# Three expert layers: token rows by indirect DMA throughout, TensorE's products of a pair in a written order, and the overflow branch moved ahead of the pairs

## The chip, the cores and the metric

The kernel runs on one core of a Trainium2 chip (trn2). The metric is the device time of one execution in microseconds (us), taken as the median of several runs; lower is better. All inputs and the output are 32-bit floats.

## What is computed

Two transformer blocks and a third one on a batch of 256 latent and 256 context tokens, 1024 wide. Each block is a mixer (attention or convolution) followed by a layer of 32 experts. The three expert layers are what the change touches:

```python
def hier_moe(h, w_group, b_group, w_expert, b_expert, w1, w3, w2):
    ...
    e_prob, e_idx = lax.top_k(jax.nn.softmax(le, axis=-1), TOP_K)
    weights = g_prob * e_prob / jnp.sum(e_prob, axis=-1, keepdims=True)
    expert_id = g_idx * EXPERTS_PER_GROUP + e_idx
    ...
    def expert_block(args):
        xb, e = args
        return (jax.nn.silu(xb @ w1[e]) * (xb @ w3[e])) @ w2[e]
    ...
    return jnp.zeros_like(h).at[stok].add(y)
```

A token goes to two experts of one group. Each expert multiplies its tokens' rows by W1 and W3 (1024 x F), takes silu(first) times second, multiplies by W2 (F x 1024), and its result, weighted, is added to the token; a gate vector scales the sum before the residual add. The first layer (moe0) has 512 tokens and F = 512, the second (moe1) 256 tokens and F = 512, the third (moe2) 256 tokens and F = 256.

## The kernel before, in words

The program runs mixer_ab, moe0, mixer_c, moe1, a third mixer and moe2 one after the other. `moe` (from L583) does one expert layer, with T = 4 or 2 tiles of 128 tokens. `make_hT` makes the normed, transposed tokens; `route` (L695) makes the router's choice, a rank of each token within its expert (TensorE products at L727, L728 and L734 into bank O), and from it the table `slot`: for each of 16 pairs of experts 128 slots (64 for each expert, `CAP`), each with a token's number and its weight. `warm` (L254) issues products whose result nobody reads.

Then come 16 turns of `pair` (L834), one for each pair of experts. Expert 0 of the pair sits in columns 0 to 63 of TensorE, expert 1 in columns 64 to 127, so that W1, W3 and W2 products run in a tile mode 64 columns wide (`128*64` in the rows below). All others (transposes, one-hot products) use the full `128*128` mode. One pair is: W1 and W3 products (`up`, L845, into the two `pj` banks), silu on ScalarE (L853), the elementwise product on VectorE (L855), its transposes (L861, bank O) and their copy (L218 on VectorE or L220 on ScalarE in turn), W2 products (L875, banks PT), a split of the weighted result into a high and a low part (L880 on ScalarE, L881 on VectorE), and `combine`: one-hot products that take the 128 slots back to the tokens (L888, 2 for each tile of tokens and half of the row, into the two banks S), the gate on VectorE (L890) and the add to the residual `xs` (L891, GpSimd for one half of the row and VectorE for the other).

How a pair gets its rows depends on the layer. In moe0 an indirect DMA on GpSimd's queue (`gather_rows`, L642) fetches the 128 slots' rows from a copy `hd` in DRAM into one half of tile `xg`, two pairs ahead, and `turn` (L650) transposes them on TensorE in 8 pieces through bank acc. In moe1 and moe2 `gather` (L808) makes one-hot matrices on VectorE (L816, L817) and multiplies them with the tokens in a high and a low part on TensorE (L824, for two pairs at a time), and scales while copying out (L225, L227).

The order on an engine is that of a list scheduler that simulates the program. `combine` of a pair is a generator; the next pair calls it through `fill` between its own products (after every 8 of W1 and W3, 2 times ahead of the transposes, 8 times ahead of W2), and the scheduler then moves the single products further, so L888 and L845 stand mixed on TensorE.

The weights come as loads of 1 MB on SyncE's queue (L200), 12 for a pair in moe0 and moe1, 6 in moe2, in the order of their use, into a cycle of buffers (7 of tag w, 7 of tag x in moe0 and 6 in the others, 1 of tag r). A load waits until the products that read its buffer are done; 11 loads (moe0) or 13 are issued ahead of the pairs.

Behind the 16 pairs stands `rest` (L896): a value is loaded into the registers of all engines (`over`, L899), and a branch (L900) enters a loop for experts that have more than 64 tokens. On these inputs it is not entered.

## Time and profile before

| what | value |
|---|---|
| median of 3 runs | 2130.99 us (2127.89 to 2133.66) |
| the profiled execution's own time | 2128.83 us |
| its span in the trace | 2126.8 us |
| mean granted TensorE clock | 0.969 |
| TensorE products busy | 1944.7 us, 91% of the span |
| TensorE weight loads busy | 998.4 us, 47% |
| VectorE, ScalarE, GpSimd busy | 1025.1, 472.5, 475.1 us |
| DMA | 635.23 MB, mean 299 GB/s |
| loops over pairs: moe0, moe1, moe2 | about 375 to 888, 1198 to 1687, 1841 to 2114 us |

Busy is the time in which an engine had an instruction of its kind running. The granted clock is a share of full speed: 1.00 is 2.4 GHz, 0.50 is 1.2 GHz. The DMA share is how much of the time the core's 16 DMA engines had packets under way; it can come out slightly above 1. The share of a whole span is an average over stages with different limits, so the rows below are cut to the three loops and to what lies between them.

### The profile page before, as it was taken

How to read it: one execution, taken by the hardware profiler on the slowest of the kernel's cores; microseconds unless marked ns; L12 is line 12 of the kernel's file. 1: busy time of each engine (PE TensorE's matmuls, PEld its weight loads, DVE VectorE, ACT ScalarE, POOL GpSimd, SP SyncE). 2: the span in 40 equal slices, each digit the busy share in tenths (PEclk: the TensorE clock that was granted, in tenths of full speed). 3: DMA queues.
4: the chain of work that ended last, by engine and by line, in shares of the span. 5: the costliest groups of instructions: out<-in, count | busy, mean ns of one | idle time of the engine just before them, and what ended most of it. 6: DMA issues, size and time to landing. Idle time of an engine off the chain costs nothing. (4 is left out here: it accounts for less than half of the span.)

```text
span 2126.8 us, 25665 instructions
## 1 busy us (share of the span) xinstructions
PE 1944.7 (91%) x9834; PEld 998.4 (47%) x9834; DVE 1025.1 (48%) x2174; ACT 472.5 (22%) x978; POOL 475.1 (22%) x387
## 2 busy tenths in 40 slices
PE   5999997999999999889988999999999797999997
PEld 2865455333333333378855533333333274555553
DVE  4567655244443434566577333322323376454544
ACT  3346522110000000133342211101111136211111
POOL 3421331121212211354244100001000125111111
PEclk7999998999999999899999999999999999999999
DMA  8645566899999999334366699999999722698882
GB/s 335 248 170 190 179 237 246 337 419 417 393 394 383 386 386 399 130 104 164 134 251 227 276 420 422 421 420 383 406 405 388 282 77 111 241 396 353 362 365 92
DMA packets 111650, 635.23 MB, mean 299 GB/s; under 512 B 12328, under 2 KB 32024, under 8 KB 40848
## 3 DMA queue, kind: packets, MB, share of 16 engines
q1 hardware_dynamic: 104608, 618.57, 73.2%
q0 software_dynamic: 4640, 8.70, 1.2%
q10 hardware_dynamic: 2256, 6.09, 0.8%
q8 instruction: 83, 1.36, 0.3%
q14 instruction: 63, 0.52, 0.1%
HBM read 634.23 MB, written 3.27 MB: 300 GB/s over the span
## 5 line engine op out<-in xcount | busy, mean ns | idle before, releaser
L891 POOL TENSOR_TENSOR xs<-xs,m 128x512 f32<-128x512 f32 x128 | 170.9, 1335 | 1031.6 <-DVE m L890 1023.2
L845 PE MATMUL pj<-w,a 128*64 128x512 f32 (+1 forms) x1592 | 381.2, 529 | 3.5 <-DVE a L225 2.8
L845 PE MATMUL pj<-x,a 128*64 128x512 f32 (+1 forms) x1296 | 331.8, 526 | 2.1 <-DVE a L225 2.1
L247 PE MATMUL pj<-w,x 128*128 128x256 f32 (+1 forms) x1728 | 285.3, 309 | 7.2 <-DVE x L234 3.0
L890 DVE TENSOR_TENSOR m<-S,bc 128x512 f32<-128x512 f32 x256 | 169.4, 684 | 179.3 <-PE S L888 176.6
L247 PEld LDWEIGHTS pj<-w,x 128*128 128x128 f32 x1728 | 230.0, 192 | 50.6 <-issue 30.1
L845 PEld LDWEIGHTS pj<-w,a 128*64 128x64 f32 x1592 | 132.5, 137 | 179.8 <-issue 154.3
L881 DVE SCALAR_TENSOR_TENSOR j<-PT,slot,j 128x512 fp32r<-128x512 f32 x96 | 71.7, 749 | 264.5 <-ACT j L880 260.4
L875 PE MATMUL PT<-x,a 128*64 128x512 f32 x608 | 185.5, 614 | 7.3 <-DVE a L218 4.3
L888 PE MATMUL S<-j,a 128*128 128x512 f32 x512 | 176.5, 443 | 16.8 <-DVE m L890 12.8
L845 PEld LDWEIGHTS pj<-x,a 128*64 128x64 f32 x1296 | 114.6, 136 | 143.8 <-issue 124.6
L875 PE MATMUL PT<-w,a 128*64 128x512 f32 x576 | 162.4, 608 | 7.9 <-DVE a L218 4.4
L855 DVE TENSOR_TENSOR a<-a,pj 128x512 f32<-128x512 f32 (+1 forms) x48 | 42.9, 894 | 232.6 <-PE pj L845 232.6
L888 PEld LDWEIGHTS S<-j,a 128*128 128x128 f32 x512 | 83.1, 190 | 147.0 <-issue 58.2
L880 ACT ACTIVATE j<-PT,slot 128x512 fp32r<-128x512 f32 x96 | 66.0, 687 | 386.4 <-PE PT L875 383.7
L891 DVE TENSOR_TENSOR xs<-xs,m 128x512 f32<-128x512 f32 x128 | 120.9, 945 | 2.5
L853 ACT ACTIVATE a<-pj 128x512 f32<-128x512 f32 (+1 forms) x48 | 25.3, 526 | 379.6 <-PE pj L845 379.6
L875 PEld LDWEIGHTS PT<-x,a 128*64 128x64 f32 x608 | 58.1, 139 | 91.4 <-issue 78.6
L875 PEld LDWEIGHTS PT<-w,a 128*64 128x64 f32 x576 | 51.2, 138 | 85.1 <-issue 70.5
L824 PEld LDWEIGHTS S<-a,x 128*128 128x128 f32 x512 | 64.4, 189 | 34.6 <-issue 11.6
L824 PE MATMUL S<-a,x 128*128 128x256 f32 x512 | 76.3, 293 | 3.0 <-DVE a L817 1.2
L263 POOL TENSOR_TENSOR sj<-sj,neghalf 128x8 f32<-128x8 f32 (+3 forms) x30 | 46.2, 1543 | 133.8 <-DVE sj L262 124.4
(363 smaller groups left out, 2430.8 us busy)
## 6 DMA issues: line engine op xcount, KB each, us to landing
w<-in_w_dram SPq DMA_DIRECT2D x189, 1024.0 KB, 9.1
x<-in_w_dram SPq DMA_DIRECT2D x170, 1024.0 KB, 10.0
x<-in_w_mod_dram SPq DMA_DIRECT2D x28, 1024.0 KB, 8.1
r<-in_w_dram SPq DMA_DIRECT2D x25, 1024.0 KB, 9.5
r<-in_w_mod_dram SPq DMA_DIRECT2D x20, 1024.0 KB, 4.9
w<-in_w_gate_e_dram SPq DMA_DIRECT2D x17, 1024.0 KB, 10.7
w<-in_w_up_e_dram SPq DMA_DIRECT2D x16, 1024.0 KB, 7.7
w<-in_w_down_e_dram SPq DMA_DIRECT2D x16, 1024.0 KB, 10.6
```

The lines of the kernel that those rows point to most:

```text
L247: self.nc.tensor.matmul(out, a[x], b[y], start=first and i == 0, stop=last and i == len(terms) - 1)
L263: self.nc.gpsimd.tensor_tensor(out, ms, self.neghalf[:, :cols], op=OP.pow)
L824: nc.tensor.matmul(px[:, k, :], h(t)[i][:, (k0 + k) * 128:(k0 + k + 1) * 128], oh[:, t], start=t == i == 0, stop=t == T - 1 and i == 1)
L845: nc.tensor.matmul(ph[64 * e:64 * e + 64, :], xT(k, e), W(e, k), start=(k == 0), stop=(k == 7), tile_position=(0, 64 * e))
L853: nc.scalar.activation(s, p1, AF.Silu)
L855: nc.vector.tensor_tensor(a.rearrange("p (k q) -> p q k", k=nk), s.rearrange("p (q k) -> p q k", k=nk), p3.rearrange("p (q k) -> p q k", k ...
L875: nc.tensor.matmul(py[n][64 * e:64 * e + 64, :], aT[:, k, 64 * e:64 * e + 64], W2(e, k)[:, n * 512:(n + 1) * 512], start=(k == 0), stop=(k ...
L880: nc.scalar.activation(hi, py[n], AF.Copy, scale=slot[:, 1:2])
L881: nc.vector.scalar_tensor_tensor(lo, py[n], slot[:, 1:2], hi, op0=OP.mult, op1=OP.subtract)
L888: nc.tensor.matmul(po, back[:, t * 128:(t + 1) * 128], parts[n][i], start=(i == 0), stop=(i == 1))
L890: nc.vector.tensor_tensor(tmp, po, gate[:, n * 512:(n + 1) * 512], op=OP.mult)
L891: (nc.vector if n and (DVA or last) else nc.gpsimd).tensor_tensor(xn, xn, tmp, op=OP.add)
```

## The change

Rows: moe1 and moe2 fetch their rows by indirect DMA as well; the one-hot `gather` and all that fed it (`kp`, the high and low parts in `make_hT`) go. `route` hands back its work in pieces: the count `over` at once, then `ids` (the token numbers of all slots, tile `at`), then `weigh`; the table with the weights is built by `table`.

Branch: `rest` stands between the first two gathers and the 16 pairs. The branch is an edge that no instruction of an engine is moved across by the scheduler, and it put all gathers behind the branch.

Order: with `tc.keep_in_program_order` the products of a pair stand as written. With T = 2: W1, W3, the previous pair's combine (8 products, banks S, S, acc, O), the transposes, the turn of the next pair's rows, W2. With T = 4 the combine is cut in two, 8 products behind W1 and 8 behind W3. A change of mode is a step from `128*64` to `128*128` products or back.

Smaller parts: with T = 2 the gate is multiplied into the pair's result before the split, and VectorE adds the combine's bank straight to `xs`; the copy of the transposes is always ScalarE's; moe1 and moe2 issue 12 loads ahead in place of 13, and their cycle has 7 buffers of tag x.

```diff
-        self.cycle = ["w"] * TAGS["w"][1] + ["x"] * (TAGS["x"][1] - (T if T == 2 else 1)) + ["r"] * TAGS["r"][1]
+        self.cycle = ["w"] * TAGS["w"][1] + ["x"] * (TAGS["x"][1] - 1) + ["r"] * TAGS["r"][1]
...
+            ids()
+            xg = self.t("x").rearrange("p (b d) -> p b d", b=2)
+            nc.gpsimd.memset(xg, 0.0)
+        ahead(8 - T // 2 * (3 if T == 2 else 2))
...
+        for p in range(2):
+            gather_rows(self.at[:, p:p + 1], xg[:, p])
+        weigh()
         add = [(self.xs[:, t], gates[i // 2]) for i, t in enumerate(tiles)]
+        self.rest(m, T, inputs, over, experts, add)
+        xT = turn(xg[:, 0], "aa")
+        self.slot = self.cp.tile([128, 16, 2], F32, name=f"slot{m}", tag="slot")
+        self.table(T, 0, self.slot)
         done = iter(())
         for p in range(16):
-            if T == 2 and p and p % 2 == 0:
-                xT = pairs(p)
-            if T > 2:
-                if p + 2 < 16:
-                    gather_rows(self.slot[:, p + 2, 0:1], p % 2)
+            if p + 2 < 16:
+                gather_rows(self.at[:, p + 2:p + 3], xg[:, p % 2])
+            after = {}
+
+            def meanwhile():
                 if p + 1 < 16:
-                    xT[p + 1] = turn((p + 1) % 2)
...
+                    after["xT"] = turn(xg[:, (p + 1) % 2], pin=self.tc.keep_in_program_order)
...
         run(done)
-        self.rest(m, T, inputs, over, experts, add)
...
+        def ids():
             chosen(rank2, each(rank))
...
+            self.at = self.cp.tile([128, 16], I32, name=f"at{m}", tag="at")
+            nc.vector.tensor_scalar(self.at, self.tokens(T, R.rearrange("p w t e -> p (w t) e"), 0), -1.0, None, op0=OP.add)
...
+        pin = (lambda i: i) if lean else tc.keep_in_program_order
...
         p1 = up(W1)
         s, a = self.t("a2", FF), self.t("a2", FF)
         nc.scalar.activation(s, p1, AF.Silu)
+        if T > 2:
+            step()
         p3 = up(W3)
...
-        fill()
-        fill()
-        pa = self.p("O", FF).rearrange("p (k s) -> p k s", k=nk)
+        step()
+        pa = self.p("pj", FF).rearrange("p (k s) -> p k s", k=nk)
...
-        self.copy(aT, pa)
+        self.copy(aT, pa, "a")
+        meanwhile()
...
+        one = T == 2
         for n in range(2):
             hi, lo = parts[n]
-            nc.scalar.activation(hi, py[n], AF.Copy, scale=slot[:, 1:2])
-            nc.vector.scalar_tensor_tensor(lo, py[n], slot[:, 1:2], hi, op0=OP.mult, op1=OP.subtract)
+            if one:
+                y = self.t("m2")
+                nc.vector.scalar_tensor_tensor(y, py[n], slot[:, 1:2], add[0][1][:, n * 512:(n + 1) * 512], op0=OP.mult, op1=OP.mult)
+                nc.scalar.activation(hi, y, AF.Copy)
+                nc.vector.tensor_tensor(lo, y, hi, op=OP.subtract)
...
+            units = [(t, n) for t in range(T) for n in range(2)]
+            for u0 in range(0, 2 * T, 4):
+                run4 = list(zip(units[u0:u0 + 4], [self.p(b) for b in ("S", "S", "acc", "O")]))
+                for (t, n), o in run4:
                     for i in range(2):
...
+                        pin(nc.tensor.matmul(o, back[:, t * 128:(t + 1) * 128], parts[n][i], start=(i == 0), stop=(i == 1)))
```

On TensorE in moe1, inside W1 and W3 of one pair, the order before was as follows (pj_11007 is the bank of W1, pj_11039 that of W3, j the high and low parts, S the combine's bank; a `64x512` row is a product in the narrow mode):

```order
L845 MATMUL pj_11039<-w_10993,a_2599_10937 64x512
L845 MATMUL pj_11039<-w_10995,a_2600_10938 64x512
L845 MATMUL pj_11039<-w_10997,a_2600_10938 64x512
L845 MATMUL pj_11039<-w_10995,a_2600_10938 64x512
L888 MATMUL S_11016<-j_10903,a_2591_10899 128x512
L888 MATMUL S_11030<-j_10904,a_2591_10899 128x512
L888 MATMUL S_11030<-j_10905,a_2591_10899 128x512
L845 MATMUL pj_11039<-w_10997,a_2600_10938 64x512
L845 MATMUL pj_11039<-w_10995,a_2600_10938 64x512
L845 MATMUL pj_11039<-w_10997,a_2600_10938 64x512
L845 MATMUL pj_11039<-w_10995,a_2600_10938 64x512
L845 MATMUL pj_11007<-x_10985,a_2599_10937 64x512
```

The combine's rows L888 stand in the middle of a pair's products, in groups of 1 to 4. The same place of the changed kernel, behind 32 rows L812 of W1 and W3 (L862 is the combine, L827 the transposes, L635 the turn of the next pair's rows, L840 W2):

```order
L862 MATMUL S_12411<-j_12316,a_2920_12313 128x512
L862 MATMUL S_12411<-j_12317,a_2920_12313 128x512
L862 MATMUL S_12412<-j_12318,a_2920_12313 128x512
L862 MATMUL S_12412<-j_12319,a_2920_12313 128x512
L862 MATMUL acc_12413<-j_12316,a_2920_12313 128x512
L862 MATMUL acc_12413<-j_12317,a_2920_12313 128x512
L862 MATMUL O_12414<-j_12318,a_2920_12313 128x512
L862 MATMUL O_12414<-j_12319,a_2920_12313 128x512
L827 MATMUL pj_12427<-cst,a_2943_12391 128x128 x4
L635 MATMUL S_12435<-cst,x_10646 128x128 x4
L635 MATMUL S_12441<-cst,x_10646 128x128 x4
L840 MATMUL PT_12454<-r_12365,a_2950_12432 64x512
```

All products in the wide mode now stand in one piece between W3 and W2.

On TensorE at the start of moe1's pairs the order before was this (L824 is the one-hot gather of the first two pairs, L899 the load of `over`, L845 W1 of the first pair):

```order
L824 MATMUL S_10648<-a_2534_10626,x_10470 128x256
L824 MATMUL S_10648<-a_2534_10626,x_10471 128x256
L824 MATMUL S_10648<-a_2534_10626,x_10470 128x256
L824 MATMUL S_10648<-a_2534_10626,x_10471 128x256
L899 TENSOR_LOAD over_10689
L254 MATMUL acc_13763<-cst 128x512 x4
L845 MATMUL pj_10734<-w_10456,a_2535_10635 64x512
L845 MATMUL pj_10734<-w_10458,a_2535_10635 64x512
L824 MATMUL S_10659<-a_2534_10626,x_10470 128x256
```

The changed kernel has there, from the last row of the branch's body on (L885, L882 and L880 are the branch's own, L778 a part of the weight table, L635 the turn of the first rows, L812 W1 of the first pair):

```order
L862 MATMUL O_11264<-j_11226,a_2649_11220 128x512
L885 REGISTER_ALU
L885 COMPARE_AND_BRANCH
L885 UNCONDITIONAL_BRANCH
L882 UNCONDITIONAL_BRANCH
L880 UNCONDITIONAL_BRANCH
L778 MATMUL pj_11302<-j_11303,a_2670_11297 64x16 x8
L635 MATMUL S_11278<-cst,x_10646 128x128 x4
L635 MATMUL S_11284<-cst,x_10646 128x128 x4
L812 MATMUL pj_11317<-w_10451,a_2666_11277 64x512
```

The first pair's products now stand behind the branch and behind the turn, which reads what the first gather brings; on GpSimd's queue that gather (L627) also stands behind the branch (L880).

## Rows read from the trace of the kernel before

**Rows 1.** Windows: us, busy time of PE, PEld, DVE, ACT, POOL, granted clock, DMA share, GB/s
```profile
391.00:880.00 489.00, 466.32 (x1866) 171.38 (x1864) 200.63 (x321) 43.12 (x68) 95.68 (x73) 1.00 0.96 386
1215.00:1440.00 225.00, 211.50 (x916) 82.19 (x913) 73.86 (x132) 25.44 (x41) 17.91 (x14) 0.99 1.01 421
1440.00:1665.00 225.00, 209.16 (x882) 80.09 (x882) 71.73 (x125) 23.49 (x38) 20.44 (x16) 0.98 0.98 395
1850.00:2085.00 235.00, 226.03 (x1434) 125.77 (x1431) 118.99 (x238) 41.72 (x76) 33.32 (x26) 1.00 0.90 367
```

**Rows 2.** Timeline of PE in the first loop: start, us, then idle before and releaser
```profile
642.78 7.09 PE L845 MATMUL pj<-x,a 128*64 128x512 f32 x32
651.10 0.66 PE L861 MATMUL O<-cst,a 128*128 128x128 f32 x4 [1.23 <-DVE a L855]
651.71 0.63 PE L650 MATMUL acc<-cst,x 128*128 128x128 f32 x4
```

**Rows 3.** Timeline of PE in the second loop: one pair's W2 products
```profile
1338.11 7.14 PE L875 MATMUL PT<-w,a 128*64 128x512 f32 x32 [0.79 <-DVE a L218]
```

**Rows 4.** Groups by line, 1215 to 1680: the one-hot gather's products
```profile
L824 PE MATMUL S<-a,x 128*128 128x256 f32 x224 | 32.7, 292 | 0.6 <-DVE a L225 0.6
```

**Rows 5.** Chain of waits in the third loop: two products of a combine
```profile
1948.07 0.67 PE S L888 x2
```

**Rows 6.** Timeline of PE in the third loop: W1 and W3, half the width
```profile
2105.34 3.67 PE L845 MATMUL pj<-x,a 128*64 128x256 f32 x32
```

**Rows 7.** DMA, 400 to 850: GpSimd's queue, and its gathers' time to landing
```profile
q0 software_dynamic: 1728, 2.97, 1.8%
...
x<-hd,sg POOLq DMA_INDIRECT x12, 8.3
```

**Rows 8.** Timelines of POOL, PE and SP's queue at the first loop's start
```profile
367.15 1.14 POOL L642 DMA_INDIRECT x<-hd,sg  x1 [29.29 <-DVE sg L641]
...
371.84 1.09 PE L650 MATMUL acc<-cst,x 128*128 128x128 f32 x4 [5.96 <-DMA x<-hd,sg]
...
374.76 1.98 PE L845 MATMUL pj<-w,a 128*64 128x512 f32 x4
...
380.13 0.81 SPq L200 DMA_DIRECT2D w<-in_w_dram  x2
```

**Rows 9.** Timelines of PE and DVE at the second loop's start
```profile
1187.65 0.36 PE L728 MATMUL O<-j,cst 128*128 128x32 f32 x2
...
1190.80 0.41 DVE L791 TENSOR_SCALAR a<-cst,rank 128x64 f32<-128x64 f32 x2
...
1198.26 1.08 PE L845 MATMUL pj<-w,a 128*64 128x512 f32 x4
```

**Rows 10.** Chain of waits at the third loop's start
```profile
1833.77 0.21 PE O L728 x2
...
1842.57 1.01 PE pj L845 x8
```

**Rows 11.** Instructions of line L900: ns least/median/most, then first and last start
```profile
L900 PEldq COMPARE_BRANCH  x3: 3295/3617/3997, 902.8 to 2118.3; - x3
...
L900 DVEq COMPARE_BRANCH  x3: 63/63/72, 905.3 to 2120.3; - x3
...
L900 DVEq EVENT_SEMAPHORE  x3: 21/21/21, 908.2 to 2120.8; - x3
```

**Rows 12.** Timelines of PE and ACT at the ends of the three layers
```profile
879.52 8.83 PE L875 MATMUL PT<-x,a 128*64 128x512 f32 x32 [0.78 <-DVE a L218]
...
908.82 1.06 ACT L356 ACTIVATE a<-xs 128x1024 f32<-128x1024 f32 x1 [6.42 <-DVEq L900]
...
1682.92 4.08 PE L875 MATMUL PT<-x,a 128*64 128x512 f32 x17
...
1695.88 1.06 ACT L356 ACTIVATE a<-xs 128x1024 f32<-128x1024 f32 x1 [8.16 <-DVEq L900]
...
2110.79 3.65 PE L875 MATMUL PT<-x,a 128*64 128x512 f32 x16 [0.56 <-DVE a L218]
```

More of the change, by code (lines that the diff above doesn't have):

```diff
@@ L57, in _constants @@
     add("fold", np.tile(np.eye(64)[:, :36], (2, 1)))
-    add("pair", np.broadcast_to(np.repeat(np.arange(16) * 128.0, 1), (128, 16)))
     return np.concatenate(blocks, axis=1)
@@ L125 @@
 DVA = True
-NA = 7
 class Experts:
@@ L652, in turn, with inputs @@
             return lambda k, e: xT[:, k, e * 64:e * 64 + 64]
-        if T == 2:
-            pairs = lambda p: self.gather(T, h, [lambda j, q=q: kp[:, j, q:q + 1] for q in (p, p + 1)], col)
-            xT = pairs(0)
-            over = table()
-            inputs = lambda sl, kc: self.gather(T, h, [lambda j: kc[:, j:j + 1]], col)[0]
-        else:
-            for p in range(2):
-                gather_rows(self.slot[:, p, 0:1], p)
-            xT = {0: turn(0)}
-            def inputs(sl, kc):
-                gather_rows(sl[:, 0:1], 0)
-                return turn(0)
+        def inputs(sl):
+            rows, at = self.t("a4"), self.sm(1, "sg", I32)
+            nc.vector.tensor_copy(at, sl[:, 0:1])
+            nc.gpsimd.memset(rows, 0.0)
+            gather_rows(at, rows)
+            return turn(rows)
@@ L679, in moe @@
+            done = self.pair(m, T, xT, E[p].start(), self.slot[:, p], add, lambda: next(done, None), meanwhile, last=p == 15)
+            xT = after.get("xT")
         run(done)
-        self.rest(m, T, inputs, over, experts, add)
     def first_of(self, T, n, v, mx):
@@ L834, in pair @@
-    def pair(self, m, T, xT, weights, slot, add, fill, lean=False, last=False):
+        st = self.p("pj", 16)
+        rv = self.t("j", n * NE)
+        nc.vector.tensor_tensor(rv.rearrange("p (w t e) -> p w t e", w=2, t=T), R.rearrange("p (w t) e -> p w t e", w=2), by,
+                                op=OP.mult)
+        rv = rv.rearrange("p (i q a) -> p i a q", i=n, a=2)
+        for a in range(2):
+            for i in range(n):
+                nc.tensor.matmul(st[64 * a:64 * a + 64], oh[:, i], rv[:, i, a], start=i == 0, stop=i == n - 1,
+                                 tile_position=(0, 64 * a))
@@ new lines, in by_slot, with tokens, table @@
+        return st
+    def tokens(self, T, R, r):
+        token = self.c("token")[:, :T].rearrange("p (w t o) -> p w t o", w=1, o=1).to_broadcast([128, 2, T, NE])
+        return self.by_slot(T, R, r, token)
+    def table(self, T, r, slot):
+        nc = self.nc
+        R = self.t("j", 2 * T * NE).rearrange("p (i e) -> p i e", e=NE)
+        for i in range(2 * T):
+            nc.vector.tensor_scalar(R[:, i], self.c("ekey"), self.base2[:, i:i + 1], None, op0=OP.is_equal)
+        if r:
+            nc.vector.tensor_scalar(slot[:, :, 0], self.tokens(T, R, r), -1.0, None, op0=OP.add)
+        else:
+            nc.vector.tensor_copy(slot[:, :, 0], self.at)
+        weight = self.pay.rearrange("p (w t o) -> p w t o", w=2, o=1).to_broadcast([128, 2, T, NE])
+        nc.vector.tensor_copy(slot[:, :, 1], self.by_slot(T, R, r, weight))
@@ L837, in pair @@
+    def pair(self, m, T, xT, weights, slot, add, step=lambda: None, meanwhile=lambda: None, lean=False, last=False):
         nc, tc = self.nc, self.tc
```

186 lines of the change are left out of this document (55 added, 131 removed).

## The prediction

> **What bounds the kernel now.** I read the windows first, cut to the three loops over pairs. In the first loop TensorE is busy 466.32 of 489 us while the DMA share is 0.96; in the second 211.50 of 225 and then 209.16 of 225 us at a share of 1.01 and then 0.98; in the third 226.03 of 235 us at 0.90 [rows 1]. So two limits lie close together: TensorE's products and the stream of weights. The reader should see that in the first half of the second loop the transfers are saturated, at 421 GB/s, and that in its second half the rate is 395 GB/s: there TensorE hands back buffers too late, and the stream stutters. The second view, TensorE's timeline, says what a pair's products cost; the third, the starts and ends of the layers, what lies between the loops.
>
> **Price of the stream.** A load is 1.0486 MB; at 421 GB/s [rows 1] that is 2.49 us. Twelve make 29.9 us for a pair in the first two loops, six make 14.9 us in the third. An indirect gather is on the same 16 DMA engines: 12 of them took 1.8% of 450 us [rows 7], 0.68 us each with 512 tokens. It moves 0.25 MB, the rows of occupied slots; with 256 tokens half as many slots are occupied, so I estimate 0.34 us.
>
> **Price of TensorE's products after the change.** W1 and W3 are 7.09 us each [rows 2], W2 7.14 [rows 3], four transposes 0.66, eight transposes of the next rows 2 x 0.63 [rows 2]. Two combine products take 0.67 us [rows 5], so the 8 of T = 2 take 2.7 and the 16 of T = 4 5.4 us. With T = 2 this is 14.2 + 7.1 + 0.7 + 1.3 + 2.7 = 26.0 us; with T = 4 28.6 us. In the third layer W1 with W3 is 2 x 3.67 [rows 6], W2 3.65 [rows 12], two transposes some 0.4: 7.3 + 3.7 + 0.4 + 1.3 + 2.7 = 15.4 us. What goes with T = 2 is the one-hot gather: 224 products in 32.7 us [rows 4], 16 of them a pair, 2.3 us, against 1.3 for the turn: 1.0 us a pair less, and with it VectorE's one-hots and the affine copies.
>
> **Price of the changes of mode.** The trace has no row for one. Lower bound nothing, since the mixed products of the loops keep TensorE busy 93% to 96% [rows 1]. Upper bound all the idle time there, 13.5 of the 225 us of the second loop's first window, which hold 7.4 pairs at the 30.5 us worked out below: 1.8 us a pair. I take it inside a pair's waits, below. The Trainium skill, "TensorEngine Tiling (Array Packing)", section Key Properties, says that a change of tiling mode drains TensorE, and gives no price; by that rule the fixed order, with fewer changes, could only gain where TensorE is the limit, and no row shows a drain by itself.
>
> **Waits that the written order could open.** The transposes need VectorE's product of the pair; before, TensorE stood 1.23 us ahead of them [rows 2]. Now 2.7 us of combine lie there and cover it. ScalarE's copy of the transposes (0.79 us of wait before W2 [rows 3]) is covered by the turn, 1.3 us. The gather is issued one pair ahead of its turn and lands in 8.3 us [rows 7], less than the shortest pair. If these covers failed, 1.23 + 0.79 = 2.0 us a pair would come back.
>
> **First layer.** The loop now runs from 374.76 to 879.52 + 8.83 = 888.35 [rows 8, 12]: 513.6 us, 32.1 a pair. After: 192 loads less 15 buffers leave 177, 441 us; the first of them issues 5.4 us after the first product (374.76 to 380.13 [rows 8]); 14 gathers add 9.5; the last load lands after 2.5 us and W2's remainder is some 5. Together 463 us. TensorE alone needs 16 x 28.6 = 458 plus a half-speed start of some 4: 462. Two limits as near as this get in each other's way, as 395 against 421 GB/s in the second loop show [rows 1], so I add 7: 470, a gain of 43.5. The start changes little: rank to first gather loses the weight part of the table, the branch gives it back: -2. At the end, 888.35 to 908.82 is 20.5 us [rows 12]. The branch there costs 2.9 us on VectorE's sequencer (905.3 to 908.2) and 3.3 to 4.0 on TensorE's [rows 11], and the last combine gets four banks in place of two: -7.5, between -3 (the branch alone) and -12. Layer: **-53**.
>
> **Second layer.** The loop runs from 1198.26 to 1682.92 + 4.08 = 1687.0 [rows 9, 12], 488.7 us, 30.5 a pair. After: first reload 7 us in, 441, 14 gathers 4.8, 2.5 and 5: 460; TensorE, at 16 x 26 = 416, is no limit. I take 462, a gain of 27. The start gets longer, since it is now serial. From the rank product to the first product it is 1198.26 - 1187.65 = 10.6 us now [rows 9]. After: token table 4.6 (the rank's one-hots began 3.2 us behind the rank product, at 1190.80 [rows 9], and eight small products follow), load of `over` and branch 3.5 (TensorE's median 3.6 [rows 11]), gather until its rows are there 371.84 - 367.15 = 4.7, turn at half speed 2 x 1.09 and its copies [rows 8] about 3: 16 us, **+5.5**; bounds +1 (branch hidden beside the table) and +10. The end, 1687.0 to 1695.88 [rows 12], is 8.9 us; split 1.5 and combine 2.7 and a last add stay: -4. Layer: **-25.5**.
>
> **Third layer.** 1842.57 [rows 10] to 2110.79 + 3.65 = 2114.44 [rows 12], 271.9 us or 17.0 a pair. The stream needs only 81 loads, 202 us, so TensorE sets it: 16 x 15.4 = 246, and I add 0.5 a pair for waits: 254, a gain of 18 (bounds: nothing added, 246; 2.0 a pair added, 278). The start, 1833.77 to 1842.57 [rows 10], is 8.8 us and becomes 15: +6. At the end the branch overlaps the output's DMA: -1. Layer: **-13**.
>
> **Sum.** -53 - 25.5 - 13 = -91.5 against the profiled execution's 2128.83 (its span of 2126.8 and 2.0 around it): 2037.3 us. The median shown is 2.2 us above that execution, so I forecast **2040 us**. Less than 0.3%, some 6.4 us, could not be told from no change.
>
> **Rival 1, the stream is the limit already.** A share of 1.01 in the second loop and 0.96 in the first [rows 1] speaks for it: if the DMA engines serve no more than now, the second loop gains nothing (27 less) and the first at most 4%, 20 us (23 less). That gives 2040 + 50 = 2090 us. Against it: the rate fell from 421 to 395 GB/s within one loop at nearly the same share, so the share also counts waiting. Chance 0.18.
>
> **Rival 2, the covers fail.** If 2.0 us a pair comes back, the second loop hides it (28.0 under 30.3), the first goes to 30.6 a pair on TensorE and loses some 10 us by it, the third to 278 us, 24 more: 2040 + 34, about 2075 us. For it: VectorE now runs the combine's adds ahead of other work, and TensorE's products cannot step around a late one. Chance 0.17.
>
> **Rival 3, slower: the clock.** With TensorE faster than the stream in the first two loops, it waits for loads in every pair, some 2 us in the first and 4 in the second. Where it idled long ahead of a layer its granted clock was lower: the four transposes took 1.09 us at 371.84 against 0.63 in the loop [rows 8, 2]. If each pair's waits brought a quarter of its products back to 1.2 GHz, a pair would cost 25% more: 35.8, 32.5 and 19.3 us, and the loops 573, 520 and 308 us against 470, 462 and 254: 215 more, about 2255 us. The loss begins where h, the share of products at half speed, makes the gain of 91 good: around 0.14 in all three. Against it: 0.99 to 1.00 was granted in three of the four windows, also in the one with a saturated stream [rows 1], and the waits are spread over the 12 loads. The Trainium skill, "TensorE: Matmul & The Clock Gate", section HAM oscillation, describes this pattern, products shorter than the wait for the next load, so that each group starts cold. By that rule the time would be that of this rival; so far the trace disagrees, with 0.99 at 1.01 of DMA share. Chance 0.05.
>
> **Rival 4, more gain.** If the near limits don't disturb each other, and the starts cost nothing extra: 7 + 8 + 11 less, about 2012 us. Chance 0.07.
>
> That the change doesn't do what it says is out: the order printed above shows the combine in one piece and the branch ahead of the pairs.
>
> **How the numbers follow.** The forecast has 0.53, and its own range is 2022 to 2060 (the bounds of starts and ends). 2008 to 2095 takes in rivals 1, 2 and 4 for the most part, and leaves out rival 3 and the tails: about 0.8. All cases but rival 3 lie more than 6.4 us below the time before, save a far end of rivals 1 and 2 together: faster 0.93, same 0.03, slower 0.04.
>
> **What would show it.** Right: in windows of the first two loops the DMA share near 1.0 at about 420 GB/s throughout, TensorE's busy time below 0.9 of the second loop, pairs of 29 to 31 us; in the third, pairs near 15.7 and waits ahead of the transposes and W2 below 0.5 us; 15 to 17 us from the rank product to W1 in moe1 and moe2; no L899 or L900 time between the layers. Wrong: waits for VectorE ahead of the turn or the transposes in every pair (rival 2), a rate under 400 GB/s at a share of 1 (rival 1), a granted clock under 0.95 inside a loop (rival 3), or a start longer than 21 us.

## The result and the profile after

The changed kernel takes 2013.72 us (median of 4 runs, 2009.85 to 2016.10) where the kernel before takes 2129.72 beside it: ratio 0.945, 95% interval 0.944 to 0.946, 116 us less. The profiled execution took 2014.55 us, with a span of 2012.7. The forecast was 2040, its range 2008 to 2095: the direction and the range held, the gain was 25 us larger than forecast, and the narrower range of 2022 to 2060 us was missed by 8 us.

The windows of the changed kernel, cut to its three loops (columns as in [rows 1]; the second loop has two windows as there):

```profile
391.00:830.00 439.00, 418.39 (x1859) 167.24 (x1856) 201.91 (x294) 47.53 (x75) 87.53 (x71) 1.00 1.01 420
1215.00:1440.00 225.00, 198.19 (x898) 74.83 (x894) 58.21 (x96) 23.82 (x39) 7.94 (x8) 1.00 1.01 420
1440.00:1605.00 165.00, 138.53 (x620) 51.21 (x617) 36.38 (x60) 15.86 (x26) 2.98 (x3) 1.00 1.01 421
1790.00:1990.00 200.00, 197.99 (x1404) 118.68 (x1406) 97.79 (x172) 38.37 (x73) 13.12 (x13) 1.00 1.01 419
```

The rate is 420 GB/s throughout, also where it was 386, 395 and 367 before [rows 1]. TensorE's busy share in the second loop fell to 88% and then 84%, while in the third it is 99%: the first two loops now go at the pace of the stream, the third at TensorE's (experiment 2 shows it). The third loop's transfers run at 419 GB/s too: six loads of 2.49 us are 14.9 us a pair, more than TensorE now needs, so it uses up what was loaded ahead, and its last four pairs wait for loads (14.3 to 15.5 us each).

What TensorE waits for in the second loop, from 1156 to 1620 (us in total, times, longest wait):

```profile
PE pj L812 <- DMA x<-in_w_dram: 24.0, 23, 1.3
PE pj L812 <- DMA w<-in_w_dram: 23.1, 21, 1.3
...
PE pj L827 <- DVE a L822: 1.2, 1, 1.2
PE PT L840 <- DMA w<-in_w_dram: 0.8, 4, 0.2
PE PT L840 <- ACT a L217: 0.7, 1, 0.7
```

The waits are for loads: 47.1 us in these two rows in 44 pieces of at most 1.3 us, and 53.5 us in 58 pieces of at most 1.4 with the smaller rows for tag r and for W2. The waits for VectorE ahead of the transposes and for ScalarE ahead of W2 occur once, in the first pair, which has no previous combine. Before, they stood in nearly every pair of this loop (1199 to 1687):

```profile
PE O L861 <- DVE a L855: 16.5, 15, 1.2
PE PT L875 <- DVE a L218: 5.9, 7, 1.2
PE PT L875 <- ACT a L220: 4.8, 7, 0.7
```

In the third loop before, the first of them did not occur, and TensorE waited 1.4 us in all ahead of W2.

One pair of the third loop in the chain of waits (start, us, what):

```profile
1794.81 6.91 PE pj L812 x64
1801.71 1.12 PE S L862 x4
1802.84 0.46 PE acc L862 x2
1803.29 0.47 PE O L862 x2
1803.77 0.22 PE pj L827 x2
1803.99 0.87 PE S L635 x8
1804.86 3.58 PE PT L840 x16
1808.44 6.91 PE pj L812 x64
```

Nothing but TensorE's products, one behind the other: 1808.44 - 1794.81 = 13.64 us a pair (the difference of the unrounded times). All pairs up to the 12th take this.

The starts: in the second layer the rank product and the first W1 product on TensorE's timeline, and between them the chain:

```profile
1142.11 0.36 PE L714 MATMUL O<-j,cst 128*128 128x32 f32 x2
...
1155.97 12.30 PE L812 MATMUL pj<-w,a 128*64 128x512 f32 x49 [0.17 <-ACT a L217]
```

```profile
1137.14 9.98 DMA hd<-x
...
1147.94 5.79 DMA x<-hd,at
...
1153.87 1.10 PE S L635 x4
```

The write of the rows to DRAM (`hd`) is under way for 10 us, then the gather for 5.8. The rank product to W1 takes 13.9 us here (10.6 before [rows 9]).

The third layer's start, and the ends of the three layers (last W2 products, then the next stage's first transposes L362):

```profile
1765.30 0.36 PE L714 MATMUL O<-j,cst 128*128 128x32 f32 x2
...
1780.66 8.45 PE L812 MATMUL pj<-w,a 128*64 128x256 f32 x64
```

```profile
837.03 5.36 PE L840 MATMUL PT<-x,a 128*64 128x512 f32 x22 [0.34 <-DMA x<-in_w_dram]
...
864.62 0.27 PE L362 MATMUL S<-cst,a 128*128 128x128 f32 x1
...
1614.96 5.36 PE L840 MATMUL PT<-x,a 128*64 128x512 f32 x22 [0.37 <-DMA x<-in_w_dram]
...
1627.97 0.27 PE L362 MATMUL S<-cst,a 128*128 128x128 f32 x1
...
2000.51 3.65 PE L840 MATMUL PT<-w,a 128*64 128x512 f32 x16 [0.47 <-ACT a L217]
```

The same transposes in the kernel before began here (its W2 ended at 888.35 and 1687.0 [rows 12]):

```profile
916.43 0.27 PE L369 MATMUL S<-cst,a 128*128 128x128 f32 x1
...
1699.19 0.45 PE L369 MATMUL S<-cst,a 128*128 128x128 f32 x1 [8.61 <-DVE sa L262]
```

In the third layer before, the rank product and the first W1 product stood here:

```profile
1833.61 0.36 PE L728 MATMUL O<-j,cst 128*128 128x32 f32 x2
...
1840.77 0.65 PE L845 MATMUL pj<-w,a 128*64 128x256 f32 x4
```

The prediction took the later 1842.57 [rows 10], which is the second group of W1 products, so the third start before was 7.2 us and not 8.8, the third loop 273.7 us and not 271.9.

From these rows, and the first layer's first W1 product at 376.45 (374.76 before [rows 8]), the account in us (differences of unrounded times):

| part | forecast | measured |
|---|---|---|
| up to the first layer's W1 | -2 | +1.7 |
| first loop, 513.6 to 465.9 | -43.5 | -47.6 |
| its end, W2 to transposes, 28.1 to 22.2 | -7.5 | -5.9 |
| mixer_c, transposes to rank, 271.2 to 277.5 | 0 | +6.3 |
| second start, 10.6 to 13.9 | +5.5 | +3.3 |
| second loop, 488.7 to 464.3 | -27 | -24.4 |
| its end, 12.2 to 7.6 | -4 | -4.6 |
| third mixer, 134.4 to 137.3 | 0 | +2.9 |
| third start, 7.2 to 15.4 | +6 | +8.2 |
| third loop, 273.7 to 223.5 | -18 | -50.2 |
| last W2 to the end, 12.3 to 8.5 | -1 | -3.8 |
| sum | -91.5 | -114.1 |

One line is far off: the third loop. Other runs that leave the starts as they are say how much a single start varies: 20.4 to 21.7 us from rank product to W1 in the first layer, 13.5 to 14.0 in the second, 12.6 to 15.5 in the third.

### The profile page after: what moved, and what is told of

It is laid out like the page before. It is cut to its first block, busy times and chain, and to the rows that moved or that the text cites. A ratio compares the mean times of both kernels' runs of the same rounds, so it can differ in the third digit from the quotient of the medians.

```text
span 2012.7 us, 24999 instructions
## 1 busy us (share of the span) xinstructions
PE 1812.4 (90%) x9610; PEld 958.5 (48%) x9610; DVE 957.4 (48%) x1988; ACT 466.9 (23%) x980; POOL 413.3 (21%) x353
## 3 DMA queue, kind: packets, MB, share of 16 engines
HBM read 651.00 MB, written 5.37 MB: 326 GB/s over the span
## 4 chain that ended last, share of the span: by engine, by line
DMA 45%; PE 26%; DVE 6%; issue 3%; POOL 1%; ACT 1%; DVEq 0%; another core or an unknown queue 0%; POOLq 0%; SPq 0%; ACTq 0%
DMA x<-in_w_dram 18%; DMA w<-in_w_dram 18%; PE pj L812 8%; PE pj L244 4%; PE PT L840 4%; DMA w<-in_w_up_e_dram 2%; DMA r<-in_w_dram 2%; DVE x L1138 1%; PE S L991 1%; DMA x<-hd,at 1%; PE S L862 1%; DMA w<-in_w_in_c_dram 1%; DMA hd<-x 1%; DMA x<-in_w_gate_e_dram 1%; PE S L635 1%
## 5 line engine op out<-in xcount | busy, mean ns | idle before, releaser
L812 PE MATMUL pj<-w,a 128*64 128x512 f32 (+1 forms) x1568 | 357.3, 528 | 33.8 <-DMA w<-in_w_dram 31.8
L812 PE MATMUL pj<-x,a 128*64 128x512 f32 (+1 forms) x1360 | 311.9, 528 | 33.2 <-DMA x<-in_w_dram 32.5
L812 PEld LDWEIGHTS pj<-w,a 128*64 128x64 f32 x1568 | 133.5, 139 | 213.1 <-issue 121.7
L812 PEld LDWEIGHTS pj<-x,a 128*64 128x64 f32 x1360 | 111.8, 137 | 201.3 <-issue 118.1
L627 POOL DMA_INDIRECT x<-hd,at x48 | 48.9, 1019 | 630.9 <-PE S L635 553.2
L840 PE MATMUL PT<-x,a 128*64 128x512 f32 x616 | 169.8, 598 | 5.1 <-DMA x<-in_w_dram 3.6
L871 POOL TENSOR_TENSOR xs<-xs,m 128x512 f32<-128x512 f32 x64 | 82.8, 1294 | 353.8 <-DVE m L870 353.8
L840 PE MATMUL PT<-w,a 128*64 128x512 f32 x544 | 146.4, 598 | 2.1 <-DMA w<-in_w_dram 1.7
L217 ACT ACTIVATE a<-pj 128x512 f32<-128x512 f32 (+1 forms) x48 | 25.3, 527 | 446.3 <-PE pj L827 446.3
L870 DVE TENSOR_TENSOR m<-S,bc 128x512 f32<-128x512 f32 x64 | 41.2, 681 | 115.7 <-PE S L862 115.7
L840 PEld LDWEIGHTS PT<-x,a 128*64 128x64 f32 x616 | 49.2, 136 | 94.8 <-issue 77.5
L848 DVE SCALAR_TENSOR_TENSOR m<-PT,slot,bc 128x512 f32<-128x512 f32 x64 | 48.0, 750 | 95.1 <-PE PT L840 95.1
L818 ACT ACTIVATE a<-pj 128x512 f32<-128x512 f32 (+1 forms) x48 | 25.3, 527 | 266.7 <-PE pj L812 266.7
L862 PE MATMUL S<-j,a 128*128 128x512 f32 x256 | 79.5, 427 | 6.3 <-ACT j L852 2.2
L849 ACT ACTIVATE j<-m 128x512 fp32r<-128x512 f32 x64 | 40.3, 630 | 180.7 <-DVE m L848 180.7
L840 PEld LDWEIGHTS PT<-w,a 128*64 128x64 f32 x544 | 42.6, 136 | 78.9 <-issue 66.7
L871 DVE TENSOR_TENSOR xs<-xs,m 128x512 f32<-128x512 f32 x64 | 78.5, 1226 | 2.0
L380 DVE TENSOR_REDUCE sa<-S 128x1 f32<-128x512 f32 (+1 forms) x96 | 57.5, 599 | 32.6 <-PE S L991 16.4
## 6 DMA issues: line engine op xcount, KB each, us to landing
w<-in_w_gate_e_dram SPq DMA_DIRECT2D x17, 1024.0 KB, 10.9
```

Of the source, the lines that this page charges most:

```text
L380: nc.vector.tensor_reduce(mx, S, axis=AX.X, op=OP.max, negate=True)
L627: nc.gpsimd.indirect_dma_start(out=out, out_offset=None, in_=hd[:], in_offset=bass.IndirectOffsetOnAxis(ap=at, axis=0), bounds_check=T * 1 ...
L812: pin(nc.tensor.matmul(ph[64 * e:64 * e + 64, :], xT(k, e), W(e, k), start=(k == 0), stop=(k == 7), tile_position=(0, 64 * e)))
L840: pin(nc.tensor.matmul(py[n][64 * e:64 * e + 64, :], aT[:, k, 64 * e:64 * e + 64], W2(e, k)[:, n * 512:(n + 1) * 512], start=(k == 0), sto ...
L848: nc.vector.scalar_tensor_tensor(y, py[n], slot[:, 1:2], add[0][1][:, n * 512:(n + 1) * 512], op0=OP.mult, op1=OP.mult)
L849: nc.scalar.activation(hi, y, AF.Copy)
```

## The experiments

Loops and starts are measured as in the account, from the first W1 to the end of the last W2 product, and from the rank product to W1. Pairs are the distances between the transposes of one pair and the next.

**1. The order alone taken back.**

```diff
-        pin = (lambda i: i) if lean else tc.keep_in_program_order
+        pin = lambda i: i
...
-                    after["xT"] = turn(xg[:, (p + 1) % 2], pin=self.tc.keep_in_program_order)
+                    after["xT"] = turn(xg[:, (p + 1) % 2])
```

> The changed kernel with TensorE's products of a pair left to the scheduler's order; everything else stays (rows by indirect DMA, branch in front, four banks for the combine). Theory A (the first two loops go at the pace of the weight stream, the third at TensorE's): the scheduler puts combine products straight behind W2, where they wait for the split (0.75 + 0.64 + 0.70 us at the end of the changed kernel), so a pair of the third loop goes from 13.64 us to about 16 and that loop from 223.5 to about 260; the first two loops hide most of it, at most 10 us each. Sum 30 to 55 us slower than the changed kernel. Rival B (the rows by DMA made the gain, the order nothing): within 6 us of the changed kernel.

Measured: 2076.41 us, ratio 0.975 (0.973 to 0.977), 63 us slower than the changed kernel. Loops 495.4, 466.1 and 255.9 us. The rows by DMA and the rest of the change thus bring 18, 23 and 18 us in the three loops (against 513.6, 488.7 and 273.7), the order 29.5, 1.7 and 32.4; how the first share divides between the rows and the smaller parts was not tried. In the second loop theory A holds. In the first it failed: the stream hides nothing there, since TensorE's pairs took 31.3 to 33.4 us, above the stream's 30.5. Its waits in that loop:

```profile
PE pj L827 <- DVE a L822: 15.7, 14, 1.2
PE PT L840 <- ACT a L217: 8.9, 13, 0.7
```

These 24.6 us are the two waits that the kernel before had [rows 2, 3]. They are not all: against the 419.6 us that TensorE needs for this loop in the written order (experiment 2) it took 76 us more. From the timeline, TensorE changed its mode 143 times in this loop, in place of 63; at experiment 3's 0.26 us the 80 more are an estimated 21 us. And the clock has a share:

```profile
704.61 7.14 PE L840 MATMUL PT<-x,a 128*64 128x512 f32 x32 [0.69 <-ACT a L217]
...
734.93 0.66 PE L827 MATMUL pj<-cst,a 128*128 128x128 f32 x4 [1.19 <-DVE a L822]
736.27 5.37 PE L840 MATMUL PT<-w,a 128*64 128x512 f32 x16 [0.69 <-ACT a L217]
741.45 3.65 PE L840 MATMUL PT<-x,a 128*64 128x512 f32 x16
```

Behind the same two waits as in the pair before, half of W2 took 5.37 us in place of 3.65: the granted clock was 1.00 up to 736 us, 0.68 from 736 to 738, 0.50 from 738 to 740 and 0.97 from 740 to 742. Five pairs of this loop, every second one from the sixth on, took 33.4 us in place of 31.7 so, 8.5 us in all. What is left of the 76 us was not split.

In the third loop the scheduler's pairs 3 to 6 took 13.6 us, as in the written order, the later ones 16.0 to 19.2. The time is near theory A's 260 us, but its wait, for the split (L849 and L850), was 6.2 us of the 32.4; waits ahead of W2, the transposes and W1 make 8.1 more, and 36 more changes of mode an estimated 6.

**2. Half of the weights.**

```diff
-        loads = ((e, at) for e in E for at in list(e.todo))
+        loads = ((e, at) for e in E[::2] for at in list(e.todo))
...
-            done = self.pair(m, T, xT, E[p].start(), self.slot[:, p], add, lambda: next(done, None), meanwhile, last=p == 15)
+            done = self.pair(m, T, xT, E[p - p % 2].start(), self.slot[:, p], add, lambda: next(done, None), meanwhile, last=p == 15)
```

> The changed kernel with half of the weight loads left out: each odd pair multiplies with the weights of the even pair ahead of it, so the output is not the reference's. Theory A (the first two loops wait for the weight stream, the third for TensorE): all pairs go at the pace of the changed kernel's first pairs, 26.3, 24.1 and 13.64 us, loops of about 425, 390 and 219 us in place of 465.9, 464.3 and 223.5, sum some 120 us faster than the changed kernel, about 1893 us. Rival B (the written order's own waits, or the gathers, set the 30.5 us a pair): the first two loops stay within 10 us of 466 and 464.

Measured: 1878.22 us (one run). Loops 419.6, 386.6 and 218.6, and every pair at 26.31, 24.11 and 13.64. Windows in its three loops:

```profile
391.00:780.00 389.00, 387.80 (x1832) 160.88 (x1830) 201.40 (x292) 47.49 (x75) 86.11 (x70) 1.00 0.58 230
1120.00:1480.00 360.00, 358.79 (x1730) 142.17 (x1728) 106.71 (x176) 45.76 (x75) 12.86 (x13) 1.00 0.60 245
1660.00:1860.00 200.00, 200.00 (x1444) 120.20 (x1442) 98.56 (x173) 38.75 (x74) 13.08 (x13) 1.00 0.47 182
```

TensorE is busy without a gap once loads aren't late. Half of the loads are left out here, and the time is 15 us below the expected 1893. Theory A is shown: the stream costs the changed kernel 46 and 78 us in the first two loops and 5 in the third.

**3. Four more changes of mode.**

```diff
-        p3 = up(W3)
+        p3 = up(W3, () if T > 2 else (4, 10))
...
+                if n in at:
+                    step()
...
-            for u0 in range(0, 2 * T, 4):
+            for u0, u1 in ((0, 4), (4, 8)) if T > 2 else ((0, 1), (1, 2), (2, 4)):
```

> The changed kernel with four more changes of mode in each pair of the second and third layer: of the previous pair's combine one unit of 2 products behind the 4th and one behind the 10th product of W3, the other two units where all four stood. Same products, same banks. Theory A (a change of mode costs next to nothing): pair of the third loop 13.64 us within 0.1, time within 4 us. Rival B (each change drains TensorE for 0.1 to 0.4 us): 0.4 to 1.6 us a pair, third loop 6 to 25 us longer, second loop hidden under the weight stream.

Measured: 2017.40 us, ratio 0.948 (0.946 to 0.949), 3.7 us above the changed kernel, with intervals that touch; the pairs decide. Pairs of the third loop 14.34 us in place of 13.64, so 0.70 / 4 = 0.175 us a change. The second loop's first three pairs, where the stream is not yet the limit, took 25.17 in place of 24.11: 0.26 a change. The loops took 464.6 and 229.3 us: hidden in the second, 6 us in the third. The timeline has 93 changes in each of the two loops in place of 33. Rival B is right on the price. The price shows in TensorE's timeline of the third loop:

```profile
1853.53 0.73 PE L865 MATMUL S<-j,a 128*128 128x512 f32 x2
1854.20 1.52 PE L814 MATMUL pj<-w,a 128*64 128x256 f32 x12
...
1857.75 0.73 PE L865 MATMUL acc<-j,a 128*128 128x512 f32 x2
1858.32 0.63 PE L865 MATMUL O<-j,a 128*128 128x512 f32 x2
1858.79 0.38 PE L829 MATMUL pj<-cst,a 128*128 128x128 f32 x2
```

Two products with a change on both sides hold TensorE for 1854.20 - 1853.53 = 0.67 us; two amid their like, for 1858.79 - 1858.32 = 0.47. Whether the engine empties at a change, or its weight load is only no longer covered, the run does not tell apart.

**4. The covers taken away.** The products of T = 2 in another written order: combine between W1 and W3, turn behind W2.

```diff
-        if T > 2:
-            step()
+        step()
         p3 = up(W3)
...
-        step()
+        if T > 2:
+            step()
...
-        meanwhile()
+        if T > 2:
+            meanwhile()
...
         one = T == 2
+        if one:
+            meanwhile()
```

> The changed kernel with the two covers of the written order taken away in the second and third layer, same products: the previous pair's combine stands between W1 and W3 in place of behind W3, and the turn of the next rows behind W2 in place of ahead of it. Theory A (the order is worth its covers plus 0.175 us for each change of mode, as the run with four more showed): a pair of the third loop pays 0.80 us ahead of the transposes, 0.47 ahead of W2 and 4 changes, 13.64 + 0.80 + 0.47 + 0.70 = 15.6 us, third loop some 30 us longer; the second loop, at about 24.1 + 1.2 + 0.7 + 1.1 = 27 on TensorE, stays at the stream's 30.5; time 25 to 32 us slower than the changed kernel. Rival B (the order's worth lies in the combine standing in one piece, not in the covers): pair below 14.5 us, time within 12 us.

Measured: 2049.58 us, ratio 0.962 (0.960 to 0.964), 37 us slower than the changed kernel run beside it (2012.78). Third loop 266.1 us, pairs 16.52. Theory A named the right thing and left out one wait, so the loss is above its 25 to 32 us; in 200 us of the third loop, 12 pairs:

```profile
PE pj L812 <- DVE a L215: 10.9, 12, 2.5
PE pj L827 <- DVE a L821: 9.6, 12, 0.8
PE PT L841 <- ACT a L217: 6.3, 12, 0.5
```

The first is VectorE's copy of the turned rows, which W1 now waits for, 0.76 us in a usual pair. 13.64 + 0.76 + 0.80 + 0.53 + 4 x 0.175 = 16.4. The second loop stayed at 464.2 us, though its TensorE time rose to 27.3 a pair (its first six pairs).

**5. The branch back behind the pairs.**

```diff
-        self.rest(m, T, inputs, over, experts, add)
         xT = turn(xg[:, 0], "aa")
...
         run(done)
+        self.rest(m, T, inputs, over, experts, add)
```

> The changed kernel with the overflow branch back behind the 16 pairs. Theory A (the branch's 3.7 us on TensorE's queue lie beside the write of the rows to DRAM and the first gather in the second and third layer): rank product to first W1 product stays 13.9 and 15.4 us there within 1.5 us, the first layer's start gets some 4 us shorter, the ends of the layers get 3 to 5, 4 and 1 us longer; sum 2 to 8 us slower. Rival B (the branch in front costs its full time at each start): each start 3.6 us shorter, 11 in all, the ends 9 longer, sum about -2 us.

Measured: 2018.20 us, ratio 0.948 (0.947 to 0.950), 4.5 us slower. Starts 14.5, 11.8 and 10.9 us (21.7, 13.9 and 15.4 in the changed kernel), 13.8 less in all (9.7 less than in the second profile of the changed kernel, experiment 11); ends, W2 to transposes or to the end, 27.1, 14.2 and 13.5 (22.2, 7.6 and 8.5), 16.5 more. The sum came out as theory A had it, its parts did not: the branch in front costs at every start, most in the first layer, so rival B was right on the starts. Standing in front, the branch is worth these 4.5 us of the 116. The changed kernel's branch on TensorE's queue (least, median, most in ns):

```profile
L880 PEldq COMPARE_BRANCH  x3: 3441/3692/4042, 359.4 to 1769.1; - x3
```

It is about as long as behind the pairs [rows 11].

**6. The branch between the 8th and the 9th pair.**

```diff
+            if p == 8:
+                run(done)
+                done = iter(())
+                self.rest(m, T, inputs, over, experts, add)
+                xT = turn(xg[:, p % 2], "aa")
...
-                if p + 1 < 16:
+                if p + 1 < 16 and p + 1 != 8:
```

> The changed kernel with the overflow branch between the 8th and the 9th pair of each layer, the combine of the 8th pair and the turn of the 9th pair's rows around it without cover. Theory A (at either edge the branch's time is on the path; in the middle of the first two loops TensorE waits for the stream anyway): starts as with the branch behind (14.5, 11.8, 10.9 us from rank product to first W1 product), ends as in the changed kernel, the first two loops unchanged within 3 us, the third 4 to 9 us longer; sum 5 to 10 us faster than the changed kernel. Rival B (the branch also stops the loads, or the stream can't catch up): 5 to 8 us more in each loop, sum within 3 us of the changed kernel or up to 10 slower.

Measured: 2017.45 us, ratio 0.948 (0.946 to 0.949), 3.7 us above the changed kernel, at the edge of the noise. Starts 14.6, 12.2 and 13.6, but loops 470.8, 467.8 and 231.4, 4.9, 3.5 and 7.9 longer. TensorE's timeline at the third loop's branch:

```profile
1885.47 0.63 PE L866 MATMUL O<-j,a 128*128 128x512 f32 x2
1892.21 1.94 PE L635 MATMUL S<-cst,x 128*128 128x128 f32 x8 [6.11 <-DVEq L884]
1894.08 9.23 PE L816 MATMUL pj<-w,a 128*64 128x256 f32 x64
```

It stands idle for 6.1 us (10.4 in the first loop, 5.3 in the second), and W1 with W3 then takes 9.23 us, against 7.08 elsewhere: the granted clock is 0.50 from 1890 to 1898, so this part ran at 1.2 GHz, and 1.00 from 1785 to 1886 and from 1900 on. The pair at the branch takes 26.5 us in place of 13.6; 5 us of it come back, since the last four pairs now wait for no loads.

In the first two loops the branch stops the loads, as rival B has it. SyncE's queue issues none from 600.5 to 622.5 us and from 1380.7 to 1401.2, and the DMA share falls to 0.70 and 0.34 (615 to 620, 620 to 625) and to 0.58 and 0.64 (1395 to 1400, 1400 to 1405). That is an estimated 4.8 and 3.9 us without transfers, near the 4.9 and 3.5 by which these loops got longer.

**7. Loads behind the branch.**

```diff
-        ahead(8 - T // 2 * (3 if T == 2 else 2))
...
         self.rest(m, T, inputs, over, experts, add)
+        ahead(8 - T // 2 * (3 if T == 2 else 2))
```

> The changed kernel with the last 4 (first layer) or 5 weight loads ahead of the pairs issued behind the branch in place of ahead of it. Theory A (the start of the second and third layer waits for the rows' write to DRAM, 10.0 and 10.6 us from issue to landing because it shares the DMA engines with these loads): the write lands in 4 to 6 us, the first W1 product comes 4 to 6 us earlier in both, time 6 to 14 us faster. Rival B (the stream of weights is the limit, and starts five loads, 12.5 us, later): the first two loops get longer by as much as their start is shorter, or more, time 0 to 15 us slower.

Measured: 2012.75 us, ratio 0.945 (0.944 to 0.947), the same as the changed kernel. It tells nothing apart: the scheduler issued the loads ahead of the branch as before, seven x loads from 1121.95 on in the second layer.

**8. The write to DRAM ahead of the last loads.**

```diff
-        self.nc.sync.dma_start(w, src)
+        (self.ldq or self.nc.sync).dma_start(w, src)
...
+            with self.tc.issue_after(put.ins):
+                self.ldq = nc.scalar
+                ahead(5)
+                self.ldq = None
```

> The changed kernel with the last five weight loads ahead of the pairs of the second and third layer issued from ScalarE's queue behind the writes of the rows to DRAM, in place of SyncE's queue beside them. Theory A (the write shares the DMA engines with loads under way): it lands in 4 to 6 us in place of 10, the first W1 product of both layers comes 3 to 6 us earlier, sum 5 to 11 us faster. Rival B (the write's time is its own, or the branch sets the start): starts within 1.5 us, time within 4 us.

Measured: 2016.89 us, ratio 0.947 (0.945 to 0.948), not clear of the changed kernel's interval. Starts of the second and third layer 17.4 and 17.2, longer by 3.5 and 1.8 (the second of these is near what this start varies by). The gather of the second layer was issued 5.4 us behind the rank product in place of 5.8, but landed after 10.0 us in place of 5.8, and W1 came 12.0 us behind its issue in place of 8.0: the loads that stood beside the write now stand beside the gather. Neither theory had that. When the write landed the profile does not show.

**9. Experiments 6 and 8 together**, with the third layer's branch ahead of the 15th pair.

> The two edits together, with the branch of the third layer ahead of its 15th pair, where the stream has become the limit. Theory A: the gains of both add up for the most part, since with the branch out of the way the start is set by the write and the gather alone; 10 to 20 us faster than the changed kernel, 1994 to 2004 us. Rival B (both remove the same wait): no more than the better of the two alone.

Measured: 2030.11 us, ratio 0.953 (0.952 to 0.955), worse than either. The starts are 14.5, 16.0 and 16.2 where experiment 6 had 14.6, 12.2 and 13.6, so the moved loads made the second and third longer here too. The loops are 470.2, 466.8 and 236.2: the pair at the third loop's branch takes 25.3 us and the last one 16.3, with 15.0 and 14.8 in the changed kernel, so at the 15th pair little was left in which to catch up.

**10. Gathers ahead of the branch.**

```diff
-            gather_rows(self.at[:, p:p + 1], xg[:, p])
+            put = gather_rows(self.at[:, p:p + 1], xg[:, p])
...
-        self.rest(m, T, inputs, over, experts, add)
+        with self.tc.issue_after(put.ins):
+            self.rest(m, T, inputs, over, experts, add)
```

> The changed kernel with the first two gathers of each layer put ahead of the branch on GpSimd's queue. Theory A (in the first layer the gather waits only for GpSimd's branch, in the other two for the write of the rows, which lands behind the branch): first layer's first gather some 5 us earlier and its first W1 product 4 to 8 us earlier, the other starts within 1.5 us; time 3 to 9 us faster than the changed kernel. Rival B (the branch waits on every engine until the gathers under way have landed): starts 0 to 4 us longer.

Measured: 2010.49 us, ratio 0.944 (0.942 to 0.945). The first gather was issued at 359.44 in place of 365.98, and the first start fell to 17.1 us; the others were 13.6 and 15.7. **11. The changed kernel once more**, beside it: 2012.78 us, ratio 0.946 (0.944 to 0.948), starts 20.4, 13.8 and 12.7.

> The changed kernel itself once more, beside the others on the same chip: 2010 to 2017 us, third loop 13.64 us a pair.

The first layer's start is 3.3 us shorter, near theory A's 4 to 8, but the intervals of the two ratios overlap, so no gain in time is shown.

## Why the prediction was right, and where not

**First and second loop.** The forecast was 470 and 462, measured 465.9 and 464.3, and half of the weights showed the reason: without the stream's limit both are 46 and 78 us shorter. The 7 us that were added for two limits in each other's way were not there, and neither was the near tie of 463 and 462 behind them: TensorE alone needs 419.6 (experiment 2). TensorE's times were too long here as well (28.6 and 26.0 forecast, 26.31 and 24.11 measured), which cost nothing where the stream is the limit.

**Third loop.** This is the step that failed: "16 x 15.4 = 246, and I add 0.5 a pair for waits: 254". TensorE did set the loop, but a pair costs 13.64 us and no wait up to the 12th pair; the loop took 223.5 us, below the 246 that the prediction set as its bound. Two errors made 15.4. A row's duration on the timeline runs from the start of its first to the end of its last product, and the next row starts before that end: W1 and W3 as one row last 7.08 us (7.3 were summed), yet the next row starts 6.91 us on in the chain; W2 is 3.58 by that measure, not 3.65; the turn 0.87, not 1.26; the transposes 0.22, not 0.44. And the combine's 0.67 us for two products [rows 5] came from the mixed order, so it held changes of mode: 8 products in one piece take 1.12 + 0.46 + 0.47 = 2.05 us, not 2.7. The 0.67 recurs to the digit in experiment 3, where units of two stand alone. The sum of the differences of starts is 13.63. The range held because its lower end was set for rival 4; the loss of 9 us in the two mixers, for which the forecast had nothing, hid part of the 32 us that this loop gained beyond its forecast.

**Changes of mode.** The prediction put them between nothing and 1.8 us a pair, and priced them inside the waits. They are 0.175 us each in the third loop and 0.26 in the second. The upper bound was wrong: it was the idle time, but the price stands inside the rows' busy time, 0.67 in place of 0.47 us for two products. Counted on the timeline before, the second loop had 147 changes, 9.2 a pair, an estimated 2.4 us; the third had 137 and has 33 now, so 104 changes at 0.175, an estimated 18 us, are part of the 50 us that it gained. The Trainium skill, "TensorEngine Tiling (Array Packing)", section Key Properties, has a change of mode drain TensorE. Experiment 3 agrees in that each change costs time, 0.175 and 0.26 us, and does not show the drain by itself.

**Rivals.** The stream as the limit already (rival 1) fell: the rate in the first loop rose from 386 to 420 GB/s. The covers (rival 2) hold in the changed kernel, and experiments 1 and 4 show what they are worth where they fail: waits of 24.6 us in the first loop, and with the changes of mode 42.6 us in the third. The clock (rival 3) stayed at 1.00 in all four windows, though TensorE waited 53.5 us for loads in the second loop: each wait is 1.4 us or less, with products on both sides. The section HAM oscillation of "TensorE: Matmul & The Clock Gate" in the Trainium skill describes a kernel whose products between two waits for loads are shorter than the wait, so that each group starts cold. Here the products between two such waits take longer than the wait, 3.65 us for 16 of them against 1.3, and the clock stayed at 1.00, so the prediction's "this pattern" did not fit. Other waits did lower the clock: the 6.1 us at a branch (experiment 6), and in the scheduler's order the two waits of 1.19 and 0.69 us around the transposes, in every second pair (experiment 1). So part of what the written order is worth in the first loop is the clock. Rival 4, 2012 us, is close to the time, yet for the most part not by its mechanism: that the near limits don't disturb each other was right, but the starts did cost extra, and the gain came from the third loop. That its figure and the measured time agree is luck.

**Starts.** The second and third were forecast at 16 and 15 us and came out at 13.9 and 15.4, but the chain in them is not the forecast's: it runs over the write to DRAM, 10 us, and the gather, 5.8, which the forecast had at 4.7, not over the table and the branch. Two paths are near each other there. In the second profile of the changed kernel (experiment 11) the gather of the third layer landed after 3.7 us in place of 6.9, the start was 12.7 us, and the branch and the weight table stand ahead of W1: VectorE's part of the table waited for the branch on TensorE's queue:

```profile
1770.77 0.68 DVE L791 TENSOR_SCALAR j<-cst,base 128x32 f32<-128x32 f32 x4 [3.01 <-PEq L880]
```

Experiment 5 shows the branch's share. The first start was forecast shorter by 2 us; from the rank product to W1 it was 18.8 us before and is 20.4 to 21.7 now, for the branch in front of its gather (14.5 without it in experiment 5, 17.1 with the gathers ahead of it in experiment 10).

**Ends and mixers.** The ends gained 14.3 us in all where 12.5 were forecast, but most of it was given back: mixer_c takes 6.3 us longer from its first transposes to the next rank product, and the third mixer 2.9. Taken together, from the last W2 product of a layer to the next rank product, it was 299.3 and 146.6 us before and is 299.7 and 145.0 now. So of the 11.5 us that the forecast had for these two ends the time shows 1.2. In mixer_c it is so in all runs, wherever the branch stands (276.7 to 282.1 us in the written order, 290.9 behind an end of only 13.9 in experiment 1, 271.2 before), so it does not hang on the branch; the third mixer took 133.7 to 137.8 in the written order. The cause was not tried and stays open.

## What to carry to other kernels

Add a stage's times by the distance from one group's start to the next group's start, and take the price of an operation from a place where it stands among its like: a short group in a mixed order carries the price of what surrounds it. Where two limits lie within a few per cent, look at the order of the products as well as at their number: here the order was worth 63 of 116 us, by covered waits, fewer changes of mode and a clock that did not fall. When a stage gets shorter, measure it together with the next one: the next may give the gain back, as the mixers did. A branch that is never taken cost several microseconds in each of the three places where it was tried; look for what it stops, here TensorE and the queue of the loads.

## What the runs showed that was not expected

- A change of TensorE's mode costs 0.175 us among products of 256 columns and 0.26 us among products of 512 (experiment 3).
- A write of 512 KB to DRAM took 10.0 us to land beside weight loads, and when the loads were moved behind it, the gather that followed took 10.0 us in place of 5.8 (experiment 8).
- A branch not taken held TensorE for 5.3 to 10.4 us in the middle of a loop, the products behind it ran slower, 9.23 us in place of 7.08, and no load was issued for over 20 us in the first two loops (experiment 6).
- Two waits of 1.19 and 0.69 us around 0.66 us of transposes were followed by a granted clock of 0.50 in every second pair, at 1.7 us each (experiment 1), while 58 waits of at most 1.4 us among longer products were not (the changed kernel's second loop).
